# A conformer convolution whose last two channel tiles go partly to TensorE, with the layer norm's early work moved

## The chip, the core and the metric

The kernel runs on one core of a Trainium2 chip. The metric is the device time of one execution in microseconds (us). Before the change it is 2323.74 us, the median of three runs (2322.24 to 2327.69). TensorE (PE in the profile) multiplies matrices, VectorE (DVE), ScalarE (ACT) and GpSimd (POOL) work elementwise, and SyncE (SP) issues all the DMAs of this kernel from one queue.

## The reference

A trunk of two layers on 256 tokens of width 2048, float32. Layer 0 mixes tokens with a Conformer convolution module, layer 1 with stick-breaking attention; each is followed by a gated feed-forward network. Every sub-layer is normed, scaled and shifted by values made from the vector c. The change lies in layer 0's mixer:

```python
def ada_ln(c, w, b):
    mod = jax.nn.silu(c) @ w + b
    shift, scale, gate = jnp.split(mod, 3, axis=-1)
...
def conformer_conv_module(h, pw1_w, pw1_b, dw_w, dw_b, ln_g, ln_b, pw2_w, pw2_b):
    u = h @ pw1_w + pw1_b                        # 2048 -> 4096
    val, gt = jnp.split(u, 2, axis=-1)
    u = val * jax.nn.sigmoid(gt)
    u = causal_depthwise_conv(u, dw_w, dw_b)     # 31 taps per channel
    u = jax.nn.silu(layer_norm(u, ln_g, ln_b))   # over the 2048 channels
    return u @ pw2_w + pw2_b
```

## The kernel before

Activations lie transposed: 16 tiles (KD) of 128 channels x 256 tokens. The stretch in question runs from about 130 to 460 us of the profile and has four parts.

**The first product (pw1)** makes, for channel tile j, the value half and the gate half in one PSUM bank: 32 blocks of 128x128 weights per tile, 8 blocks to a "piece" of 0.5 MB. `gate_act(j)` (ACT, sigmoid) and `gate_mul(j)` (DVE) turn the bank into the tile `us[j]` (u).

**The convolution** has 31 taps. Tap 30 and the bias are one ACT instruction into PSUM (`conv_first`). The next 19 are DVE instructions that multiply and add onto it (`conv_tap`). The first 11 (`POOL_TAPS`) are products on ACT (`conv_prod`, into tiles named hl) that GpSimd adds into `ys[j]`. `conv_sum(j)` adds the two halves on DVE. A loop over c = 0..16 writes this out by hand, in steps s = 0..18: in round c stand the first half of tile c's taps, the second half of tile c-1's, `conv_sum(c-2)`, the pw1 pieces of later tiles and the sums below. Each engine executes its own instructions in the written order (`in_order`), so an instruction that waits holds up everything behind it on its engine.

**The layer norm over channels** needs sums over partitions, which TensorE makes by a product with ones (`y_sum`, `y_square_sum`). To avoid cancellation the tiles are first centred by an early mean m1 of the first M0 tiles: `gather("y0")` copies the partial sums to SBUF (ACT) and sums them (PE), `first_mean` makes m1 (ACT) and a correction dm (DVE), and `y_centre(j)` subtracts m1. After the last tile the exact mean and variance follow, then the normed tiles zh and zl (a float32 value split in two), the operands of the second product (pw2).

**Beside it** part of the scale, shift and gate values (`ada_ln`) is made on TensorE from rows of weights: a "row chunk" of 1 MB is loaded and used by four 128x32 matmuls (line 551, written to auxa), which the profile shows as 8 records. `mod_rows` is a generator; each `advance(fill, 1)` takes one chunk. `ROWS_AT` says at which (c, s) a chunk stands, `ROWS_TAIL` how many follow before pw2, and the rest is spread over the pieces of pw2 at the rate `RATES["pw2"]`. Chunk 16 ends the first group: its result is copied to SBUF by ACT ("rows", line 559). `ROWS` groups of columns of the feed-forward's shift are made from rows; the other column tiles (mt_ffn, 1 MB each) are made on DVE by one multiply-and-reduce each (`mod_reduce`, line 314), in the generator `mod_part`. Row chunks in pw2 and the mt tiles share three buffers, mraw.

In pw2 and after it a scheduler places the instructions. After pw2 the feed-forward's first product starts with 64 blocks (up00a), and the next (up00b) needs the normed tiles hh and hl that DVE, ACT and GpSimd make meanwhile.

The lines that the steps speak of (`y_sums` flushes the waiting tiles to TensorE):

```python
if c == M0 + 3:
    first_mean()
...
if s == 3 and c == M0 + 2:
    gather("y0")
...
if s == 10 and 1 < c < KD:
    y_sums(c - 2)
if s in (6, 10) and c > M0 + 2 and centred < JC:
    y_centre(centred)
```

Of the kernel before, what the change touches and what calls it, by code (L numbers as in the profile page):

```python
# [24 lines left out]
PRODUCTS = 16  # L25
# [4 lines left out]
M0 = 8  # L30
MORE_ROWS = 4
SPLIT_ROWS = 3
ROWS = 3

ROWS_AT = {**{c: (11,) for c in (2, 4, 6, 8, 10, 12)}, 13: (8, 13, 18), 14: (2, 6, 10, 14, 18), 15: (2, 6, 10, 14, 18), 16: (2, 4, 6, 7)}
ROWS_TAIL = 4

RATES = {"pw2": (0.65, 0.0), "up": (0.25, 0.25), "down": (0.4, 0.0), "qk": (0.3, 0.0), "v": (0.3, 0.0),
# [77 lines left out]
def hybrid_trunk(ctx: ExitStack, tc: tile.TileContext, cfg: Cfg, io: dict):  # L116
# [356 lines left out]
    with ExitStack() as cv:  # L473
# [119 lines left out]
        spare = [v[1] for v in htiles]  # L593
# [48 lines left out]
        conv_ps, conv_banks = {}, []  # L642

        def conv_first(j):
            if len(conv_banks) < 2:
# [3 lines left out]
                                 scale=tap(j, PADW))  # L649

# [13 lines left out]
        def conv_sum(j):  # L664
            nc.vector.tensor_tensor(ys[j], ys[j], conv_ps.pop(j), op=ALU.add)
# [12 lines left out]

        def gathered(ps):

            v = t256()
            nc.scalar.copy(v, ps[:, :T])
            return v
# [13 lines left out]
        def y_sums(j):  # L697

            waiting.append(j)
            if j in (3, 7, 11) or j >= KD - 3:  # L700
                while waiting:
                    y_sum(waiting.pop(0))

        def gather(name):

            v = gathered(st[name])
            nc.tensor.matmul(st[name][:, T:2 * T], ones_q, v, start=True, stop=name == "y0", skip_group_check=True)
# [6 lines left out]
        def y_centre(j):  # L714
            nc.vector.tensor_tensor(ys[j], ys[j], m1, op=ALU.subtract)
# [39 lines left out]
        for i in range(NH, KD):  # L755
            done = min(c for c in range(KD) if upto[c] + 2 >= (i - NH + 1) * per_pair)
            gates_at.setdefault(min(done + 2, i - 1), []).append(i)
# [7 lines left out]
        for c in range(KD + 1):  # L765
            late = gates_at.get(c, [])
            if c == M0 + 3:
                first_mean()
            squared, squares = [(j, y_square(j)) for j in squares], []
            if c < M0 + 4:  # L770
                load_rows()
            taps = [(c, s) for s in range(nd - nd // 2)] if c < KD else []
            if c > 0:
                old = [(c - 1, s) for s in range(nd - nd // 2, nd)]
                taps = [t for pair in zip(taps, old + [None]) for t in pair if t] if taps else old
            made = 0
            for s in range(nd):
                if s < len(taps):
                    j, k = taps[s]
                    conv_tap(j, POOL_TAPS + k)  # L780
                while c < KD and made < min(POOL_TAPS, (s + 1) * POOL_TAPS // (nd - 4) + 1):
# [16 lines left out]
                if s == 4:  # L798
# [3 lines left out]
                    if c == KD:  # L802
# [399 lines left out]
```

## Time and profile before

| | |
|---|---|
| runs | 2322.24, 2323.74, 2327.69 us |
| profiled execution | 2325.09 us, its span 2322.9 us |
| PE busy | 2277.3 us of the span |
| DVE, ACT, POOL busy | 1732.6, 1164.3, 263.2 us |
| moved by DMA | 603.55 MB, mean 260 GB/s |

The profiled execution is 2.2 us longer than its span, and 1.35 us above the median of the runs. Busy time of PE says little by itself, since matmuls overlap and the clock of PE changes; so the stretch is read by short windows, by the list of waits and by the timeline of each engine.

### The profile page before, as it was taken

Reading aid. Unit: us, or ns where it says so; the run is one execution under the profiler, and the core shown is the slowest. Engines: PE = TensorE matmul, PEld = TensorE weight load, DVE = VectorE, ACT = ScalarE, POOL = GpSimd, SP = SyncE. Lnnn points to the kernel's source line nnn. Section 1 sums busy time; section 2 is a strip of 40 time slices with the busy share of each in tenths; the row PEclk is TensorE's granted clock in tenths of the full one; section 3 lists DMA queues with packets and bytes.
Section 4 is the critical chain, followed back from the end, with each engine's and each line's share of the span. In section 5 each row is a group of like instructions: output and inputs, shape, how many; then the busy total and the mean of one; then the engine's idle time right before and its main releaser. Section 6 shows DMA issues by size and latency. Waiting matters only on the chain.

```text
span 2322.9 us, 44140 instructions
## 1 busy us (share of the span) xinstructions
PE 2277.3 (98%) x17850; PEld 2170.8 (93%) x17850; DVE 1732.6 (75%) x2389; ACT 1164.3 (50%) x1769; POOL 263.2 (11%) x339
## 2 busy tenths in 40 slices
PE   7999999999999999999999999999999999999997
PEld 5888578999999999999988999999999999999997
DVE  7688965988887788788876766888887545666554
ACT  2055565755543355554465555657555434555543
POOL 4057701200000000001111100111000000000010
PEclk9999899999999999999999999999999999999999
DMA  9988787587779877788866667775776555555553
GB/s 397 417 330 302 284 316 304 212 307 281 278 295 341 302 281 272 255 307 321 296 202 231 238 237 270 263 267 186 283 287 219 185 190 186 188 190 190 185 189 109
DMA packets 139166, 603.55 MB, mean 260 GB/s; under 512 B 15441, under 2 KB 15569, under 8 KB 115153
## 3 DMA queue, kind: packets, MB, share of 16 engines
q1 hardware_dynamic: 138962, 600.74, 71.3%
q8 instruction: 139, 2.28, 0.4%
q14 instruction: 65, 0.53, 0.1%
HBM read 598.58 MB, written 2.10 MB: 259 GB/s over the span
## 4 chain that ended last, share of the span: by engine, by line
PE 87%; DVE 7%; DMA 4%; ACT 1%; issue 1%; POOL 0%; SPq 0%; DVEq 0%; ACTq 0%; POOLq 0%
PE ps L286 25%; PE ps L287 25%; PE ps L288 25%; PE ps L629 4%; DMA mraw<-in_mt_mix 3%; DVE mraw L314 2%; PE auxa L551 2%; DVE wl L237 1%; PE ps L1034 1%; PE ps L1035 1%; PE ps L1036 1%; DVE auxb L652 1%; DMA mraw<-in_mt_ffn 1%; DVE hl L361 0%; DVE rstd L394 0%
## 5 line engine op out<-in xcount | busy, mean ns | idle before, releaser
L233 ACT CAST wh<-raw 128x1024 fp32r<-128x1024 f32 x688 | 720.8, 1048 | 799.8 <-PE ps L287 626.9
L237 DVE TENSOR_TENSOR wl<-raw,wh 128x1024 fp32r<-128x1024 f32 x688 | 840.6, 1226 | 362.0 <-ACT wh L233 355.0
L286 PE MATMUL ps<-hh,wh 128*128 128x256 f32 (+1 forms) x3328 | 935.4, 281 | 3.4 <-ACT hh L363 2.1
L287 PE MATMUL ps<-hl,wh 128*128 128x256 f32 (+1 forms) x3328 | 932.1, 280 | 0.0
L288 PE MATMUL ps<-hh,wl 128*128 128x256 f32 (+1 forms) x3328 | 927.6, 279 | 2.5 <-DVE wl L237 2.5
L287 PEld LDWEIGHTS ps<-hl,wh 128*128 128x128 f32 x3328 | 631.3, 190 | 0.3
L286 PEld LDWEIGHTS ps<-hh,wh 128*128 128x128 f32 x3328 | 626.0, 188 | 4.3 <-ACT hh L363 2.5
L288 PEld LDWEIGHTS ps<-hh,wl 128*128 128x128 f32 x3328 | 626.7, 188 | 2.8 <-DVE wl L237 2.7
L314 DVE CUSTOM_DVE_ANT_0 mraw<-mraw,csr 128x2048 f32<-128x2048 f32 x148 | 339.4, 2293 | 118.0 <-DMA mraw<-in_mt_mix 59.8
L287 PE MATMUL ps<-gl,wh 128*128 128x256 f32 x1408 | 395.6, 281 | 0.0
L286 PE MATMUL ps<-gh,wh 128*128 128x256 f32 x1408 | 394.4, 280 | 0.0
L288 PE MATMUL ps<-gh,wl 128*128 128x256 f32 x1408 | 393.1, 279 | 0.0
L287 PEld LDWEIGHTS ps<-gl,wh 128*128 128x128 f32 x1408 | 265.8, 189 | 0.0
L286 PEld LDWEIGHTS ps<-gh,wh 128*128 128x128 f32 x1408 | 265.0, 188 | 0.0
L288 PEld LDWEIGHTS ps<-gh,wl 128*128 128x128 f32 x1408 | 264.9, 188 | 0.0
L379 POOL TENSOR_TENSOR sumsq<-sumsq,t 128x256 f32<-128x256 f32 x56 | 58.4, 1044 | 1582.5 <-ACT t L375 1582.3
L629 PE MATMUL ps<-hh,raw 128*128 128x256 f32 x832 | 188.5, 382 | 0.0
L629 PEld LDWEIGHTS ps<-hh,raw 128*128 128x128 f32 x832 | 158.0, 191 | 27.8 <-issue 5.8
L899 DVE SCALAR_TENSOR_TENSOR t<-ps,par,t 128x254 f32<-128x254 f32 x336 | 160.5, 478 | 4.1
L652 DVE SCALAR_TENSOR_TENSOR auxb<-u,cpar,auxb 128x256 f32<-128x256 f32 x304 | 125.2, 482 | 11.2 <-ACT auxb L648 10.4
L786 POOL TENSOR_TENSOR y<-y,hl 128x256 f32<-128x256 f32 x144 | 106.8, 742 | 23.3 <-ACT hl L661 12.5
L896 ACT ACTIVATE t<-ps,par 128x256 f32<-128x256 f32 x168 | 93.9, 559 | 2.3 <-PE ps L288 2.3
(187 smaller groups left out, 2106.9 us busy)
## 6 DMA issues: line engine op xcount, KB each, us to landing
raw<-in_w_down SPq DMA_DIRECT2D x176, 512.0 KB, 4.0
mraw<-in_mt_mix SPq DMA_DIRECT2D x80, 1024.0 KB, 7.7
mraw<-in_mt_ffn SPq DMA_DIRECT2D x68, 1024.0 KB, 6.4
raw<-in_w_pw SPq DMA_DIRECT2D x96, 512.0 KB, 7.6
raw<-in_w_up01b SPq DMA_DIRECT2D x84, 512.0 KB, 5.0
raw<-in_w_up11b SPq DMA_DIRECT2D x84, 512.0 KB, 3.4
raw<-in_w_up00b SPq DMA_DIRECT2D x80, 512.0 KB, 4.8
raw<-in_w_up10b SPq DMA_DIRECT2D x80, 512.0 KB, 4.4
```

What stands on the lines that cost most here:

```text
L233: nc.scalar.copy(wh[:, :n], v[:, :n])
L237: nc.vector.tensor_tensor(wl[:, :n], v[:, :n], wh[:, :n].bitcast(F32), op=ALU.subtract)
L286: nc.tensor.matmul(o, wh[:, c], xh[kt], start=first, stop=False, skip_group_check=halves > 0)
L287: nc.tensor.matmul(o, wh[:, c], xl[kt], start=False, stop=False, skip_group_check=halves > 0)
L288: nc.tensor.matmul(o, wl[:, c], xh[kt], start=False, stop=left[nb] == 0, skip_group_check=halves > 0)
L314: nc.vector.tensor_tensor_reduce(out=v, in0=v, in1=csr, scale=1.0, scalar=0.0, op0=ALU.mult, op1=ALU.add, accum_out=macc[:, nb:nb + 1])
L379: engine.tensor_tensor(self.sum, self.sum, sq, op=ALU.add)
L629: nc.tensor.matmul(banks[j][:, nb // KD * T:(nb // KD + 1) * T], w[:, b * P:(b + 1) * P], hf[kt], start=first, stop=left[j] == 0, skip_gro ...
L652: nc.vector.scalar_tensor_tensor(conv_ps[j], us[j % UBUFS][:, k:k + T], tap(j, k), conv_ps[j], op0=ALU.mult, op1=ALU.add)
L786: nc.gpsimd.tensor_tensor(ys[c], ys[c], pr, op=ALU.add)
L896: nc.scalar.activation(y, ps[:, :T], AF.Identity, bias=pc(f"fdb{i}", nb, 1), scale=w(FW - 1))
L899: nc.vector.scalar_tensor_tensor(y[:, s:], ps[:, :T - s], w(k), y[:, s:], op0=ALU.mult, op1=ALU.add)
```

## The change

1. The last two channel tiles (`LATE` = 2, tiles 14 and 15) have 7 taps on GpSimd instead of 11 and 12 on DVE instead of 19; 11 taps are matmuls with diagonal matrices (`conv_tensor`), which ACT makes from an identity (`tap_matrix`), and one more DVE addition brings them in.
2. The first mean is taken of 6 tiles instead of 8. Its steps move: the sums to s = 4, the copy to (c, s) = (8, 12), `first_mean` to (9, 8). Eight early tiles (before ten) are centred late, and this is done on GpSimd.
3. `ROWS` 3 -> 2: 40 row chunks instead of 44, and eight mt tiles instead of four in this part of the shift. 22 chunks stand before or at the start of pw2 instead of 27. In pw2 the rate is 0.8 instead of 0.65, and the mt tiles are taken between the chunks instead of after them.
4. Product tiles of the convolution are 10 instead of 16 (`PRODUCTS`), the other six hl tiles hold tap matrices. The last gate stands at (14, 3) and (14, 5).

```diff
-PRODUCTS = 16
+LATE = 2
+LATE_POOL, LATE_PE = 7, 11
+PRODUCTS = 10
-M0 = 8
+M0 = 6
-ROWS = 3
-ROWS_AT = {... 13: (8, 13, 18), 14: (2, 6, 10, 14, 18), 15: (2, 6, 10, 14, 18), 16: (2, 4, 6, 7)}
-ROWS_TAIL = 4
-RATES = {"pw2": (0.65, 0.0), ...
+ROWS = 2
+ROWS_AT = {... 13: (8, 16), 14: (8, 10, 12, 14), 15: (2, 6, 8, 11), 16: (2,)}
+ROWS_TAIL = 5
+RATES = {"pw2": (0.8, 0.0), ...
@@ mods0
-            yield from mod_rows()
+            for _ in mod_rows():
+                yield
+                if nrow["bias"]:
+                    nrow["steps"] = nrow.get("steps", 0) + 1
+                    if nrow["steps"] > 5 and nrow["steps"] % 3 == 0:
+                        next(part, None)
             yield from part
@@
+        def tap_matrix(j, i, home):
+            diag[j, i] = home
+            nc.scalar.activation(home, ident, AF.Copy, scale=tap(j, PADW - LATE_PE + i))
+
+        def conv_tensor(j):
+            tens_ps[j] = psum_acc()[:, :T]
+            for i in range(LATE_PE):
+                k = PADW - LATE_PE + i
+                nc.tensor.matmul(tens_ps[j], diag.pop((j, i)), us[j % UBUFS][:, k:k + T], start=i == 0,
+                                 stop=i == LATE_PE - 1)
@@ conv_sum
+            if late_tile(j):
+                nc.vector.tensor_tensor(ys[j], ys[j], tens_ps.pop(j), op=ALU.add)
             nc.vector.tensor_tensor(ys[j], ys[j], conv_ps.pop(j), op=ALU.add)
@@ the loop over c and s
-            if c == M0 + 3:
-                first_mean()
-                if s == 3 and c == M0 + 2:
+                if (c, s) == (M0 + 2, 12):
+                    gather_copy("y0")
                     gather("y0")
+                if (c, s) == (M0 + 3, 8):
+                    first_mean()
-                if s == 10 and 1 < c < KD:
+                if s == 4 and 1 < c < KD:
                     y_sums(c - 2)
-                if s in (6, 10) and c > M0 + 2 and centred < JC:
-                    y_centre(centred)
+                if s in (6, 10) and c > M0 + 3 and centred < JC:
+                    y_centre(centred, nc.gpsimd)
...
+                if c == KD - 2 and s == 0:
+                    conv_tensor(KD - 2)
+                if c == KD - 2 and s == 3:
+                    sg = gate_act(KD - 1)
+                if c == KD - 2 and s == 5:
+                    gate_mul(KD - 1, sg)
...
+                if c == KD - 2 and s == nd - 1:
+                    conv_tensor(KD - 1)
```

How the instructions stand. First ACT around the early mean, before (rounds 10 and 11): hl are the convolution's products, auxb is `conv_first`, L682 the copy of the sums, L710 the mean m1.

```order
L682 COPY t<-ps 128x256
L661 ACTIVATE hl_1653<-u_254,cpar 128x256
L661 ACTIVATE hl_1657<-u_254,cpar 128x256
L661 ACTIVATE hl_1661<-u_254,cpar 128x256
L661 ACTIVATE hl_1676<-u_254,cpar 128x256
L661 ACTIVATE hl_1680<-u_254,cpar 128x256
L661 ACTIVATE hl_1684<-u_254,cpar 128x256
L648 ACTIVATE auxb<-u_255,cpar 128x256
L661 ACTIVATE hl_1696<-u_254,cpar 128x256
L661 ACTIVATE hl_1700<-u_254,cpar 128x256
L710 ACTIVATE m_271<-ps 128x256
```

The copy stands in front of `conv_first`(11), the mean after it. The same engine after the change, round 9 (the copy, L730, stands in round 8):

```order
L689 ACTIVATE hl_1585<-u_254,cpar 128x256
L689 ACTIVATE hl_1589<-u_254,cpar 128x256
L689 ACTIVATE hl_1604<-u_254,cpar 128x256
L738 ACTIVATE m_272<-ps 128x256
L689 ACTIVATE hl_1611<-u_254,cpar 128x256
L689 ACTIVATE hl_1615<-u_254,cpar 128x256
L664 ACTIVATE auxb<-u_255,cpar 128x256
```

The copy has moved some 1.5 rounds ahead; now the mean stands in front of the next `conv_first`, that of tile 10. On PE the second sum of the early mean (L734, formerly L707) stands behind the row chunk of round 8:

```order
L553 MATMUL auxa<-mrow,hot 32x512 x4
L734 MATMUL ps<-t,ones_q 128x256
L640 MATMUL ps<-hh_220,raw 128x256
L640 MATMUL ps<-hh_222,raw 128x256
L640 MATMUL ps<-hh_224,raw 128x256
```

Before, it stood between the second and third piece of round 10. Third, PE from the last pw1 block to the middle of the tail, after the change (u_259 and u_260 are the tiles 14 and 15, L676 their tap matmuls, L706 the column sums; x4 of L553 is one chunk):

```order
L640 MATMUL ps<-hh_250,raw 128x256
L553 MATMUL auxa<-mrow,hot 32x512 x4
L553 MATMUL auxa<-wh,hot 32x512 x2
L553 MATMUL auxa<-wl,hot 32x512 x2
L676 MATMUL ps<-u_259,hl_241 128x256 x2
L676 MATMUL ps<-u_259,hl_243 128x256 x2
L676 MATMUL ps<-u_259,hl_245 128x256 x2
```

```order
L553 MATMUL auxa<-mraw,hot 32x512 x4
L706 MATMUL ps<-t,ones_d 32x256
L706 MATMUL ps<-y_198,ones_d 32x256
L706 MATMUL ps<-y_199,ones_d 32x256
L706 MATMUL ps<-y_200,ones_d 32x256
L706 MATMUL ps<-y_201,ones_d 32x256
L553 MATMUL auxa<-mrow,hot 32x512 x12
L734 MATMUL ps<-t,ones_q 128x256
L718 MATMUL ps<-y_202,ones_d 128x256
```

Between the two pieces stand three sums, four chunks and tile 15's 11 tap matmuls. The three chunks in the second piece end with chunk 16. Between the last pw1 block and the first pw2 matmul there are 14 chunks (before: 21); 20 then follow inside pw2 (before: 17), by the 480th of its 768 matmuls (before: by the 672nd). ACT at the same place:

```order
L689 ACTIVATE hl_2170<-u_260,cpar 128x256
L561 COPY rows<-auxa 128x512
L689 ACTIVATE hl_2182<-u_260,cpar 128x256
L747 ACTIVATE t<-y_201 128x256
L235 CAST wh<-raw 128x1024
L730 COPY t<-ps 128x256 x2
```

The copy of chunk 16's result now stands ahead of the last product of tile 15, of a weight cast and of the two copies that the final sums on PE use.

More of the change, by code (lines that the diff above doesn't have):

```diff
@@ L29 @@
 UBUFS = 9
-M0 = 8
+M0 = 6
 MORE_ROWS = 4
 SPLIT_ROWS = 3
-ROWS = 3
-ROWS_AT = {**{c: (11,) for c in (2, 4, 6, 8, 10, 12)}, 13: (8, 13, 18), 14: (2, 6, 10, 14, 18), 15: (2, 6, 10, 14, 18), 16: (2, 4, 6, 7)}
-ROWS_TAIL = 4
-RATES = {"pw2": (0.65, 0.0), "up": (0.25, 0.25), "down": (0.4, 0.0), "qk": (0.3, 0.0), "v": (0.3, 0.0),
+ROWS = 2
+ROWS_AT = {**{c: (11,) for c in (2, 4, 6, 8, 10, 12)}, 13: (8, 16), 14: (8, 10, 12, 14), 15: (2, 6, 8, 11), 16: (2,)}
+ROWS_TAIL = 5
+RATES = {"pw2": (0.8, 0.0), "up": (0.25, 0.25), "down": (0.4, 0.0), "qk": (0.3, 0.0), "v": (0.3, 0.0),
          "o": (0.4, 0.0), "up00a": (0.0, 0.0), "qk0a": (0.0, 0.0),
@@ L592, in hybrid_trunk @@
         hf = [v[0][:, :T].bitcast(F32) for v in htiles]
-        spare = [v[1] for v in htiles]
+        spare = [v[1] for v in htiles[:PRODUCTS]]
+        homes_of_taps = [v[1][:, i:i + P].bitcast(F32) for v in htiles[PRODUCTS:] for i in (0, P)]
+        ident = homes_of_taps.pop()
+        nc.gpsimd.affine_select(out=ident, in_=ones, pattern=[[1, P]], compare_op=ALU.is_equal, fill=0.0, base=0,
+                                channel_multiplier=-1)
         act_tables("sigmoid_and_others")
@@ L699, in y_sums, with gather_copy @@
             waiting.append(j)
-            if j in (3, 7, 11) or j >= KD - 3:
+            if j in (3, M0 - 1, M0 + 3) or j >= KD - 3:
                 while waiting:
                     y_sum(waiting.pop(0))
+        def gather_copy(name):
+            st["g" + name] = t256()
+            nc.scalar.copy(st["g" + name], st[name][:, :T])
         def gather(name):
-            v = gathered(st[name])
-            nc.tensor.matmul(st[name][:, T:2 * T], ones_q, v, start=True, stop=name == "y0", skip_group_check=True)
+            nc.tensor.matmul(st[name][:, T:2 * T], ones_q, st.pop("g" + name), start=True, stop=name == "y0",
+                             skip_group_check=True)
         def first_mean():
@@ L778, in hybrid_trunk @@
                 if s < len(taps):
-                    j, k = taps[s]
-                    conv_tap(j, POOL_TAPS + k)
-                while c < KD and made < min(POOL_TAPS, (s + 1) * POOL_TAPS // (nd - 4) + 1):
+                    conv_tap(*taps[s])
+                while c < KD and made < min(pool_taps(c), (s + 1) * pool_taps(c) // (nd - 4) + 1):
                     pr = conv_prod(c, made)
```

37 lines of the change are left out of this document (25 added, 12 removed).

## The prediction

> **What bounds the kernel now.** The page shows PE busy in nearly every slice, so I read windows of 5 us from 130 to 460 us (columns: window, length, then busy time and instructions of PE, PEld, DVE, ACT and POOL, the granted clock as a share, the DMA share, GB/s) first, then the waits and the timelines of the engines where a window shows a hole.
>
> ```profile
> 225.00:230.00 5.00, 5.00 (x29) 3.81 (x28) 1.01 (x3) 0.31 (x2) 0.00 (x0) 1.00 0.72 286
> 270.00:275.00 5.00, 0.62 (x4) 0.18 (x2) 4.76 (x13) 1.16 (x4) 4.05 (x6) 0.86 1.04 421
> 275.00:280.00 5.00, 4.31 (x22) 1.28 (x20) 4.97 (x12) 4.52 (x13) 3.45 (x5) 0.50 1.02 387
> 280.00:285.00 5.00, 5.00 (x26) 2.60 (x26) 4.96 (x14) 3.15 (x8) 4.25 (x6) 0.50 0.97 388
> 285.00:290.00 5.00, 5.00 (x33) 1.66 (x28) 4.72 (x11) 0.00 (x0) 0.00 (x0) 0.77 1.03 433
> 300.00:350.00 50.00, 49.97 (x381) 40.01 (x384) 35.20 (x65) 30.43 (x50) 0.00 (x0) 1.00 0.87 335
> 435.00:440.00 5.00, 2.67 (x22) 2.43 (x20) 5.00 (x8) 4.73 (x9) 3.57 (x4) 1.00 0.18 70
> 440.00:445.00 5.00, 4.86 (x28) 4.86 (x29) 5.00 (x11) 3.03 (x8) 1.59 (x2) 0.66 0.48 150
> ```
>
> Only places where PE isn't full, or not at full clock, can give time back. At 225 DVE and ACT stand nearly still while PE is full: a stall that PE does not feel. Between 270 and 290 it is DVE that is full while PE has a hole and then half a clock. From 300 on pw2 fills PE. At 437 and after there is a second hole, again with half a clock behind it. The waits (total us, count, longest) say who is waited for, 225 to 300 first (where the copy L682 holds up ACT, and with it conv_first of tile 11), then 296 to 520:
>
> ```profile
> ACT t L682 <- PE ps L676: 16.9, 3, 9.7
> DVE auxb L652 <- ACT auxb L648: 7.9, 5, 6.9
> PE ps L676 <- ACT t L719: 4.4, 1, 4.4
> ```
> ```profile
> PE ps L288 <- DVE wl L237: 2.5, 1, 2.5
> PE ps L286 <- ACT hh L363: 1.1, 1, 1.1
> ```
>
> And the timelines (start, length) of PE and DVE:
>
> ```profile
> 220.80 1.07 PE L551 MATMUL auxa<-mrow,hot 128*32 128x512 f32 x8
> 228.90 0.64 PE L676 MATMUL ps<-y,ones_d 128*32 128x256 f32 x8
> 257.98 3.72 PE L629 MATMUL ps<-hh,raw 128*128 128x256 f32 x16
> 261.63 1.06 PE L551 MATMUL auxa<-mrow,hot 128*32 128x512 f32 x8
> 291.69 1.92 PE L551 MATMUL auxa<-mrow,hot 128*32 128x512 f32 x16
> 300.03 0.71 PE L286 MATMUL ps<-zh,wh 128*128 128x256 f32 x4 [1.35 <-ACT zh L360]
> 303.02 1.07 PE L551 MATMUL auxa<-mraw,hot 128*32 128x512 f32 x8
> ```
> ```profile
> 213.76 3.62 DVE L652 SCALAR_TENSOR_TENSOR auxb<-u,cpar,auxb 128x256 f32<-128x256 f32 x9
> 232.95 2.45 DVE L652 SCALAR_TENSOR_TENSOR auxb<-u,cpar,auxb 128x256 f32<-128x256 f32 x6 [6.94 <-ACT auxb L648]
> 290.71 0.42 DVE L715 TENSOR_TENSOR y<-y,m 128x256 f32<-128x256 f32 x1
> 295.25 0.42 DVE L841 TENSOR_TENSOR t<-ps,t 128x256 f32<-128x256 f32 x1
> ```
>
> PE ends pw1 at 261.63 and starts pw2 at 300.03. In between DVE sets the pace until tile 15 is centred at 291.13; the variance follows at 295.25, pw2 4.78 us later. So the length from 261.6 to 300.0, the chunks inside pw2 and the hole at 437 are what the change can move.
>
> **The change, part by part.**
>
> *The early mean.* The stall of 6.94 us before 232.95 goes from its place, but I expect it one round and a half earlier. The second sum of the mean (L734) now stands behind the row chunk of round 8, which PE reached at 220.80 before; PE is at L734 at 222.3 or so. DVE would reach the correction dm at about 215.7, in the middle of the nine taps that start at 213.76, and wait until about 223.4, 7.7 us. It then starts tile 11 at about 234.5, against 232.95. Behind DVE's wait stand taps only, and PE is held up by none of them before 262: 0 on the path, at most the 1.5 us of lateness if DVE stayed the bound.
>
> *DVE and POOL in the tail.* Durations from the groups of 255 to 300 (DVE) and 130 to 300 (POOL):
>
> ```profile
> L652 DVE SCALAR_TENSOR_TENSOR auxb<-u,cpar,auxb 128x256 f32<-128x256 f32 x66 | 27.9, 479 | 0.8 <-ACT auxb L648 0.5
> L715 DVE TENSOR_TENSOR y<-y,m 128x256 f32<-128x256 f32 x11 | 6.3, 570 | 0.2
> L786 POOL TENSOR_TENSOR y<-y,hl 128x256 f32<-128x256 f32 x144 | 106.8, 742 | 23.3 <-ACT hl L661 12.5
> ```
>
> DVE loses 2 x 7 taps at 27.9/66 = 0.42 us (5.9) and eight centrings at 0.57 (4.6) and gains two additions (0.8): 9.7 less, 1.5 late, so tile 15 is summed at about 282 to 283 instead of 291. POOL gains eight centrings, for which I take 0.74 each: twelve operations in a round of tile 10 or later are 9 us, a round of DVE is 9 us too, so POOL runs level, and the late tiles give it back 2 x 4 additions. Nothing waits for it longer than before by this count.
>
> *PE from pw1 to pw2.* Piece prices: a chunk is half of the 1.92 us at 291.69 less 0.2 for the trailing end, 0.87; a 128x256 product in float32 is 3.72 less 0.2 for eight, 0.44, which I take for a tap product, as its shape is the same. One group of sums more stands ahead of the last piece (the group at 228.90, 0.6 to 1.0): 262.6. Two chunks: 264.3. Eleven taps of tile 14: 269.1. Sums and four chunks: 273.1. Eleven taps of tile 15: 277.9, if ACT has its tap matrices ready. Those are 22 small ACT copies without a row; between the per-piece price of the tiny casts and of the copy below they cost 0.10 to 0.37, 2 to 8 us against 2 x 4 products saved at 0.41 (3.3); I take 0.25 (the size lies between), which has them done at 272.6, just in time, and the bad end makes PE 2 us later. Then a chunk, five sums and three chunks: 282.1. Here PE waits, because the ACT copy that feeds L734 now stands behind the result of chunk 16:
>
> ```profile
> 405.52 1.12 ACT L437 CAST hh<-v_ffn 128x2 fp32r<-128x2 f32 x11
> 278.23 0.58 ACT L559 COPY rows<-auxa 128x512 f32<-128x512 f32 x1 [0.48 <-PE auxa L551]
> 254.08 4.09 ACT L661 ACTIVATE hl<-u,cpar 128x256 f32<-128x256 f32 x10
> 281.72 0.42 ACT L719 ACTIVATE t<-y 128x256 f32<-128x256 f32 x1 [0.29 <-DVE y L715]
> 282.04 1.03 ACT L233 CAST wh<-raw 128x1024 fp32r<-128x1024 f32 x1
> 229.69 0.37 ACT L682 COPY t<-ps 128x256 f32<-128x256 f32 x1 [9.70 <-PE ps L676]
> 286.95 0.84 PE L707 MATMUL ps<-t,ones_q 128*128 128x256 f32 x2
> ```
>
> Copy of the rows, last product, square, cast, copy: 0.58 + 0.41 + 0.42 + 1.03 + 0.37 = 2.8, so L734 starts at 285.0, PE idle for 2.9. Then L734 (0.84) and, as before from the centring of tile 15 to the variance, 295.25 - 291.13 = 4.1: variance at 289.9, pw2 at 294.8. That is **-5.2**, at full clock.
>
> *The clock.* The hole of 4.38 us before left the clock at 0.86, 0.50, 0.50 and 0.77 in four windows, 1.37 x 5 = 6.9 us of a full clock. At 437 a shorter hole (2.47) gave 0.66 in one window, 1.7 us. The new gap of 2.9 lies nearer the shorter one, but sparse column sums follow it: bounds 0 and 5, taken **+2.5**.
> [...]
>
> *Chunks inside pw2.* 20 instead of 17, at 1.07 to 1.1 (303.02): **+3.3**. That is the only lasting cost of moving seven chunks behind the norm, as four of them are gone altogether.
>
> *Transfers in pw2.* PE's chunks in 300 to 350, the chunk loads in 255 to 430 (transfers, size, median us from issue to landing), and SP's waits there:
>
> ```profile
> L551 PE MATMUL auxa<-mraw,hot 128*32 128x512 f32 x61 | 11.2, 605 | 0.0
> mraw<-in_mr_ffn SPq DMA_DIRECT2D x20, 1024.0 KB, 7.5
> SPq L215 <- PE auxa L551: 79.8, 20, 9.4
> ```
>
> The fastest rows above (270, 285) moved 421 and 433 GB/s. Before, pw2 ran at 335 (row 300) and PE never waited for a load. A product costs 0.13 us: the 381 records of row 300 are 61 of 7.6 chunks, 8 small ones and 312 products, and 49.97 - 7.6 x 1.07 - 1 = 40.8. After the change, from the third chunk of pw2 to the 480th product stand loads of 16 chunks (1.05 MB), 5 mt tiles and 15 weight pieces (0.52 MB), 29.9 MB or 71 us at 420 GB/s, against 480 x 0.13 + 17 x 1.07 = 80 us of PE. But ten chunks stand between the 300th and the 480th product, 180 x 0.13 + 10.7 = 34 us of PE, and with three mt tiles and eight pieces they load 17.8 MB, 42 us, through three mraw buffers of which an mt tile holds one until DVE has reduced it. If nothing were loaded ahead, 8 us would be missing there and some 4 more from buffers that come free late: bounds 0 and 12. The load share of 0.87 at row 300 leaves little reserve, but the queue can load ahead up to its buffers: I take **+4**, a third of the way.
>
> *The hole at 437.* It comes from the mt reductions late in pw2, which hold up DVE ahead of the reciprocal of the next norm:
>
> ```profile
> 413.23 2.28 DVE L314 CUSTOM_DVE_ANT_0 mraw<-mraw,csr 128x2048 f32<-128x2048 f32 x1
> 422.97 0.47 ACT L392 ACTIVATE t<-auxb,eps_r 128x256 f32<-128x256 f32 x1 [1.99 <-PE auxb L384]
> 427.08 1.74 DVE L394 RECIPROCAL rstd<-t 128x256 f32<-128x256 f32 x1
> ```
>
> The root is ready at 423.4, the reciprocal starts 3.6 us later. After the change chunks and mt tiles are through at the 480th product of 768, some 37 us before pw2 ends, so the reciprocal starts at once: the 2.47 and the 1.7 of half clock go, **-4.1**. The 1.1 behind it waits for ACT and I leave it; with it the bound is -5.2, and 0 if DVE is late for another reason.
>
> The sum: -5.2 + 2.5 + 3.3 + 4 - 4.1 = **+0.5**. The profiled execution (2325.09 us, 2.2 outside its span) is 1.35 above the median, so 2325.6 there and **2324.2** on the scale of the median.
>
> **The rivals.**
>
> *Loads keep up and the gap is harmless* (faster). [...] -5.2 + 0 to 1 + 3.3 + 0 to 1 - 4.1 = -6 to -4.9, about 2318, down to 2316.6 with the 1.11 too. Against it: 0.87 of the engines' time is used already at a lower rate of chunks.
>
> *pw2 is bound by its loads* (slower). Place: the last ten chunks before the 480th product. Price: 9 to 12 instead of 4, so +5.5 to +8.5, and where the half clock returns during the waits 2 more: about 2331. It decides once fewer than about 8 us of work are loaded ahead when chunk 30 is due. For it: 42 us of transfers against 34 of PE. Against it: the reserve before.
>
> [...]
>
> *The stall isn't removed at all* is part of the forecast, since PE doesn't feel it either way.
>
> **How the numbers follow.** About 0.2% (4.6 us) is what a measurement of this kernel can tell from no change. Forecast 0.36, full clock gate 0.07: both within; loads keep up 0.31, faster; loads bind 0.26, slower. The likeliest alone runs from 2320 to 2328. The range for eight in ten takes most of both rivals, leaving out the far tail of each: 2315.5 to 2333.
>
> **What would show it.** Right: pw2's first product near 295 to 297; a stall of DVE of 6 to 8 us near 216 to 223, on the second use of m1; a PE gap of 2 to 4 us near 283 behind the copy of the rows; no wait for wl at the end of up00a; 20 chunks by the 480th product with single PE waits for mraw or raw that sum to about 4. Wrong: pw2 as late as 300 (tap matrices or u of tile 15 late, or a half clock through the whole tail); PE waits for loads of over 8, or none; the hole at 437 still there; POOL's centrings so slow that sums wait for them.

## The result and the profile after

The changed kernel takes 2346.82 us (median of 4 runs, 2344.18 to 2351.08) against 2324.58 beside it: a ratio of 1.0088, 95% interval 1.0074 to 1.0102. It is slower by 20.5 us by the ratio and 22.2 by the medians, where 2324.2 was forecast with a range up to 2333.0. The profiled execution took 2344.18 us, its span 2342.1, 19.2 more than before.

Windows of after, with the columns of the prediction (window, length, then busy time of PE, PEld, DVE, ACT and POOL, the granted clock, the DMA share, GB/s):

```profile
285.00:290.00 5.00, 3.66 (x22) 1.94 (x22) 1.27 (x3) 1.25 (x4) 0.24 (x1) 1.00 1.01 428
295.00:300.00 5.00, 2.83 (x22) 0.93 (x14) 4.44 (x7) 2.52 (x5) 0.00 (x0) 0.87 0.73 252
340.00:380.00 40.00, 32.27 (x245) 23.86 (x243) 20.63 (x31) 17.25 (x33) 8.98 (x8) 1.00 0.76 287
380.00:420.00 40.00, 34.74 (x217) 27.99 (x218) 21.07 (x28) 15.23 (x27) 2.50 (x3) 0.74 1.00 403
420.00:440.00 20.00, 20.00 (x173) 20.00 (x173) 18.81 (x31) 12.73 (x27) 5.08 (x4) 1.00 0.54 185
```

The same stretch of before, in one row:

```profile
340.00:420.00 80.00, 80.00 (x648) 68.35 (x648) 51.03 (x78) 47.80 (x87) 13.44 (x14) 1.00 0.80 308
```

Before, PE had neither a hole nor a slow clock between 340 and 420. After, it stands idle for 7.7 + 5.3 = 13.0 us there, and the clock is down to 0.74 in the second half; by windows of 5 us (0.56, 0.50, 0.91, 0.77, 0.50 and 0.71 from 380 to 410, each times PE's busy time) that is, by estimate, some 8.5 us of a full clock. From 340 to 380 the DMA engines are not full either (0.76), from 380 to 420 they are (1.00). So nearly the whole loss lies in the second half of pw2. PE's timeline of after tells who is waited for (a choice of rows, with the longest waits; in square brackets the idle time and who ended it):

```profile
285.94 0.70 PE L734 MATMUL ps<-t,ones_q 128*128 128x256 f32 x2 [2.64 <-ACT t L730]
297.69 0.71 PE L288 MATMUL ps<-zh,wh 128*128 128x256 f32 x4 [2.17 <-ACT zh L362]
378.19 1.07 PE L553 MATMUL auxa<-mraw,hot 128*32 128x512 f32 x8 [2.36 <-DMA mraw<-in_mr_ffn]
380.70 1.94 PE L553 MATMUL auxa<-mraw,hot 128*32 128x512 f32 x8 [1.44 <-DMA mraw<-in_mr_ffn]
397.77 1.94 PE L553 MATMUL auxa<-mraw,hot 128*32 128x512 f32 x8 [2.59 <-DMA mraw<-in_mr_ffn]
464.70 0.36 PE L288 MATMUL ps<-hh,wh 128*128 128x256 f32 x1 [1.69 <-DVE bcol L465]
475.84 0.62 PE L288 MATMUL ps<-hh,wh 128*128 128x256 f32 x3 [0.98 <-ACT hh L365]
```

The first two are the holes ahead of pw2. The next three are row chunks that had not landed, 6.4 of the 13.0 us. The rest of the 13.0 are ten waits of 0.2 to 1.3 us: 3.5 us for weights (wh, which ACT rounds from raw, and wl, which DVE makes behind it) and 2.9 for ACT, which empties the accumulators of finished tiles and copies a result of chunks. The weights' loads came late too: ACT waited for them twice for 5 us. And the load queue itself stood still, for 9 us between two chunk loads. ACT's timeline, the queue's, and the queue's waits in 300 to 400 (total, count, longest):

```profile
381.94 1.04 ACT L235 CAST wh<-raw 128x1024 fp32r<-128x1024 f32 x1 [5.08 <-DMA raw<-in_w_pw]
387.72 1.05 ACT L235 CAST wh<-raw 128x1024 fp32r<-128x1024 f32 x1 [4.74 <-DMA raw<-in_w_pw]
```
```profile
356.94 8.97 SPq L217 DMA_DIRECT2D mraw<-in_mr_ffn  x2
```
```profile
SPq L217 <- PE auxa L553: 61.3, 17, 5.6
SPq L217 <- DVE macc L316: 15.2, 4, 8.2
```

The first of these rows for before, in the same stretch (the second has no counterpart there):

```profile
SPq L215 <- PE auxa L551: 53.6, 12, 9.4
```

SP issued all loads in one order. Loads of chunks waited until PE had used the chunk before the last (L553, 61.3 us), loads of an mt tile or of the chunk behind it until DVE had reduced an mt tile (L316, 15.2 us), and the weights written behind them waited too: none were issued from 352.5 to 376.3. The 9 us at 356.94 are such a wait for DVE (8.2). DVE reached the reduction at 363.27 only, since in its order it first waited for the scale (2.95 us, until 358.68) and then had the tiles to do that the scale releases. The DMA engines were at 0.19 from 360 to 365, and full again from 375 to 380:

```profile
375.00:380.00 5.00, 1.89 (x16) 0.16 (x8) 3.35 (x4) 1.31 (x3) 0.72 (x1) 1.00 0.99 386
```

Three places show where the 19.2 us were lost. The first product of pw2 starts 2.3 us earlier than before (297.69 against 300.03), its last ends 22.5 us later (438.76 against 416.30), and the 300th product behind pw2 starts 19.8 us later (478.46 against 458.67). So pw2 took 24.8 us longer, 2.7 were gained behind it, and no more was lost after that.

### The profile page after: what moved, and what is told of

The parts are those of the page before. It is cut to its first block, busy times and chain, and to the rows that moved or that the text cites. A ratio compares the mean times of both kernels' runs of the same rounds, so it can differ in the third digit from the quotient of the medians.

```text
span 2342.1 us, 44146 instructions
## 1 busy us (share of the span) xinstructions
PE 2284.2 (98%) x17862; PEld 2177.2 (93%) x17862; DVE 1732.5 (74%) x2377; ACT 1166.9 (50%) x1783; POOL 264.3 (11%) x340
## 4 chain that ended last, share of the span: by engine, by line
PE 85%; DVE 6%; DMA 6%; issue 2%; ACT 1%; SPq 0%; POOL 0%; DVEq 0%; ACTq 0%; POOLq 0%
PE ps L288 25%; PE ps L289 25%; PE ps L290 24%; PE ps L640 5%; DMA mraw<-in_mt_mix 3%; DVE mraw L316 2%; DVE wl L239 2%; PE auxa L553 1%; DMA mraw<-in_mt_ffn 1%; PE ps L1084 1%; PE ps L1085 1%; PE ps L1086 1%; DMA mraw<-in_mr_ffn 1%; DVE hl L363 0%; DMA raw<-in_w_pw 0%
## 5 line engine op out<-in xcount | busy, mean ns | idle before, releaser
L235 ACT CAST wh<-raw 128x1024 fp32r<-128x1024 f32 x688 | 720.5, 1048 | 792.3 <-PE ps L289 618.1
L316 DVE CUSTOM_DVE_ANT_0 mraw<-mraw,csr 128x2048 f32<-128x2048 f32 x152 | 348.4, 2292 | 128.9 <-DMA mraw<-in_mt_ffn 66.3
L288 PEld LDWEIGHTS ps<-gh,wh 128*128 128x128 f32 x1408 | 264.9, 188 | 0.0
L680 DVE SCALAR_TENSOR_TENSOR auxb<-u,cpar,auxb 128x256 f32<-128x256 f32 x290 | 118.8, 483 | 4.9 <-ACT auxb L664 4.1
L815 POOL TENSOR_TENSOR y<-y,hl 128x256 f32<-128x256 f32 x136 | 99.3, 730 | 28.1 <-ACT hl L689 15.6
```

The costliest lines, as they stand in the source:

```text
L235: nc.scalar.copy(wh[:, :n], v[:, :n])
L288: nc.tensor.matmul(o, wh[:, c], xh[kt], start=first, stop=False, skip_group_check=halves > 0)
L316: nc.vector.tensor_tensor_reduce(out=v, in0=v, in1=csr, scale=1.0, scalar=0.0, op0=ALU.mult, op1=ALU.add, accum_out=macc[:, nb:nb + 1])
L680: nc.vector.scalar_tensor_tensor(conv_ps[j], us[j % UBUFS][:, k:k + T], tap(j, k), conv_ps[j], op0=ALU.mult, op1=ALU.add)
L815: nc.gpsimd.tensor_tensor(ys[c], ys[c], pr, op=ALU.add)
```

## The experiments

Each was timed beside the kernel before; the ratio to it is given with its interval. The edits are shown shortened, `...` marking what is left out. Line numbers shift by a few between the kernels: L286 to L292 are the products, L551 to L555 the chunks, L233 or L235 ACT's rounding of weights. "Planner" is the scheduler's order on PE, "program" the order in which the program is written. "Product" counts the 768 products of pw2, in the order in which PE's trace has them: the first tile of pw2 is finished at the 300th, and the code asks there for the feed-forward's whole scale, whose last row chunk is the 32nd, with two steps (two more chunks) behind it. The 32nd stands at the 192nd product before, at the 344th after.

| run | chunks before pw2, rate, PE's order in pw2 | 32nd chunk | ratio (95%) |
|---|---|---|---|
| after | 22, 0.8, planner | 344 | 1.0088 (1.0074 to 1.0102) |
| mt_after | 22, 0.8, planner, mt tiles last | 334 | 1.0062 (1.0046 to 1.0079) |
| reduce_next | 22, 0.8, planner | 344 | 1.0086 (1.0071 to 1.0101) |
| rate65 | 22, 0.65, planner | 383 | 1.0053 (1.0035 to 1.0071) |
| near25 | 25, 0.8, planner | 269 | 1.0067 (1.0051 to 1.0084) |
| near27 | 27, 0.8, planner | 193 | 1.0056 (1.0044 to 1.0068) |
| near27_65 | 27, 0.65, planner | 207 | 1.0017 (1.0008 to 1.0025) |
| near28t | 28, 0.8, planner | 167 | 1.0038 (1.0026 to 1.0049) |
| cap3 | 22, 0.8, planner, 3 buffers | 322 | 1.0105 (1.0091 to 1.0119) |
| pe_order | 22, 0.8, program | 300 | 1.0044 (1.0029 to 1.0059) |
| pe_order25_65 | 25, 0.65, program | 264 | 1.0018 (1.0008 to 1.0027) |
| pe_order_near25 | 25, 0.8, program | 216 | 0.9996 (0.9987 to 1.0006) |
| after_27 | 27, 0.65, program | 192 | 0.9999 (0.9990 to 1.0008) |
| pe28t | 28, 0.8, program | 120 | 0.9997 (0.9987 to 1.0007) |
| pe28t_65 | 28, 0.65, program | 168 | 0.9982 (0.9974 to 0.9991) |
| tail_only | as before | as before | 1.0026 (1.0015 to 1.0037) |
| before_mods | before with the rows' part | 334 | 1.0105 (1.0084 to 1.0126) |
| before_22 | before with 22 chunks | 353 | 1.0063 (1.0046 to 1.0080) |
| rows2_27 | before, two groups, program | 192 | 1.0016 (1.0003 to 1.0028) |

**Which half of the change.** Two runs split it.

```diff
 # tail_only: after, with the row chunks of before
-ROWS = 2
+ROWS = 3
-ROWS_AT, ROWS_TAIL, RATES["pw2"] and mods0 of after
+those of before
```

> The first part of the change alone: taps on TensorE, six-tile mean, centring on GpSimd, with the row chunks as before (44 chunks, 27 before pw2, rate 0.65, four mt tiles after the chunks). All theories that put the loss into pw2's loads: pw2 runs as before, without PE waits. PE then has 21 chunks and 22 tap products after the last pw1 block, seven chunks at 0.87 more than after, of which some fill the gap of 2.6: pw2 starts at 300 to 303 instead of 297.7, so the time is that of before or up to 3 us more, 2323 to 2328. A theory by which the taps or the centring cost the 20 us would have 2340 or more.

Ratio 1.0026, and no loss in the loads: the window from 340 to 420 is full, at a clock of 1.00.

```profile
340.00:420.00 80.00, 80.00 (x647) 67.48 (x647) 47.34 (x71) 45.43 (x85) 14.09 (x14) 1.00 0.80 301
```
```profile
300.60 1.20 PE L288 MATMUL ps<-zh,wh 128*128 128x256 f32 x4 [3.08 <-ACT zh L362]
438.13 0.58 PE L288 MATMUL ps<-hh,wh 128*128 128x258 f32 x1 [3.39 <-ACT wh L235]
```

pw2 starts at 300.60 against 300.03: with the same chunks, the relief of DVE buys nothing, because the 22 tap products (2 x 5.0 us) fill what PE had idle (4.38 us ahead of 274.80) and at half clock (0.50 from 275 to 285) before. The hole at the end of up00a is a little longer (3.39 against 2.47). The 6 us are more than expected. Most of them are there by the 300th product behind pw2, which starts 5.2 us later than before (463.92 against 458.67): 0.6 ahead of pw2, 2.6 inside it (about 1.7 of this is clock, at 0.91 from 300 to 320) and 2.1 behind it.

```diff
 # before_mods: before, with the rows' part of the change
-ROWS = 3
+ROWS = 2
+ROWS_AT, ROWS_TAIL, RATES["pw2"] and mods0 of after
```

> The second part of the change alone, on the kernel before: two row groups instead of three, 22 row chunks before pw2 instead of 27, rate 0.8, mt tiles between the chunks; the convolution and the centring as before. If the loss lies in pw2's loads: pw2 starts near 300 as before (DVE sets the tail) and loses the same 20 us and more, 2342 to 2350. If the loss came from the tail's changes: near 2325.

Ratio 1.0105: the rows' part alone has the whole loss (the intervals of the two overlap). Its trace has 12.0 us of idle PE between 340 and 420, against 13.0 in after and none before. So the loss comes with the rows' part and lies in pw2.

**Do the mt tiles hold the buffers?**

```diff
 # mt_after: after, in mods0
-            for _ in mod_rows(): yield; ... next(part, None)
+            yield from mod_rows()
             yield from part
```

> The kernel after, with one thing undone: the eight mt tiles of the feed-forward's shift are again taken after the row chunks and not between them; everything else (taps on TensorE, two row groups, rate 0.8) stays. Theory H (held buffers): an mt tile sits in one of the three mraw buffers until DVE reduces it one mt step later (10.7 to 18.8 us in the trace after), the load queue stops behind it, and weights and chunks come late. Then the PE waits of 350 to 400 us (12.8 us, and about 10 us of half clock behind them) go, and the hole at the end of up00a (about 4 us) may return: 2324 to 2330. Theory R (row chunks alone are too many too soon: 20 by the 480th product through two buffers, three of them in a row): the waits for chunks stay, 2338 to 2345.

```diff
 # reduce_next: after, mod_part reduces one step after its load
-                    if nrow["steps"] > 5 and nrow["steps"] % 3 == 0:
+                    if nrow["steps"] > 5 and nrow["steps"] % 3 in (0, 1):
```

> The kernel after, with the same loads in the same order, but each mt tile is reduced on DVE one chunk step after its load instead of three. Theory H (buffers held by unreduced mt tiles stop the load queue): a tile is held some 8 us less, most of the waits in 350 to 400 go, 2328 to 2336. Theory R (row chunks alone are too many too soon): no change within 3 us, 2344 to 2350. A third possibility, that DVE itself is held up by a reduction whose tile has not landed, would make it slower than after.

mt_after: 1.0062. PE's idle time in 340 to 420 falls from 13.0 to 5.8 and the clock there rises to 0.96, but the mt tiles now end at 442, and PE waits for the shift:

```profile
445.94 0.80 PE L288 MATMUL ps<-hh,wh 128*128 128x258 f32 x2 [7.67 <-ACT hh L439]
```

So the mt tiles between the chunks are part of the loss, and moving them back loses most of it again. reduce_next: 1.0086, no change; its trace says why it tells nothing. DVE's reductions stand at 339.85, 364.82 and 379.08, as in after (338.25, 363.27, 377.53): each is 1.5 us later, as is the start of pw2 (299.31 against 297.69, 1.6 later). The experiment did not change what it meant to change.

**Is it the rate, the lateness of the scale, or the planner's order?** Four runs, of which each takes away one cause, and the last all three:

```diff
 # rate65: after
-RATES = {"pw2": (0.8, 0.0), ...
+RATES = {"pw2": (0.65, 0.0), ...
 # near25: after
-15: (2, 6, 8, 11), 16: (2,)}
+15: (2, 6, 8, 11, 12, 13, 14), 16: (2,)}
 # pe_order: after
+        here = len(nc.cur_bb.bb.instructions)
         gemm("pw2", ..., pw2_done, halves=8)
+        in_order(here, (nc.tensor.engine,))
 # pe_order25_65: the three together
```

> The kernel after with 25 row chunks before pw2 instead of 22: three more stand behind chunk 16, in the 2.6 us in which PE waits for ACT, and 18 are left for pw2; mt tiles between the chunks, rate 0.8. Theory B (burst): the first finished tile of pw2 (about the 300th product) needs the whole scale, that is 32 chunks; with 22 before pw2 they are not there yet, so the missing ones are loaded one behind the other through two buffers and the weights behind them in the queue come late. With 25 nothing is missing at that point: most of the 12.8 us of PE waits and 10 us of half clock go, 2325 to 2330. Theory Q (the rate of 0.8 with mt tiles between asks for more than the queue can move): waits stay, 2338 to 2345. Theory P (the planner puts chunks on PE ahead of where their loads stand in the queue): waits partly stay, since three chunks still stand together near the 450th product, 2333 to 2342.

> The kernel after with one number undone: the rate of row chunks in pw2 is 0.65 again instead of 0.8; two row groups, 22 chunks before pw2, mt tiles between the chunks. Theory Q (the rate asks too much of the queue): 2326 to 2334. Theory B (burst of chunks that the first finished tile needs): the burst is one chunk longer, the waits stay or grow, 2343 to 2352. Theory P (planner's order on PE against the order of the loads): four chunks stand together on PE instead of three, 2343 to 2352 too.

> The kernel after, with PE's instructions inside pw2 kept in the order in which the program writes them (the loads already are), so no chunk stands on PE ahead of the place that its load has in the queue; the three chunks that the first finished tile asks for stand together at the 300th product. Theory P: the waits for chunks go, 2326 to 2334. Theory B: the burst and the queue's order are the same, the waits only move ahead to the 300th product, 2340 to 2350. Theory Q: the same waits, 2340 to 2350.

> Three things together: PE in the program's order inside pw2, 25 chunks before pw2, rate 0.65. By each of the theories B, P and Q its own cause is gone, so all expect no PE wait of weight in pw2: the start of pw2 as after or 1 us later, 18 chunks, the hole at the end of up00a gone or shorter if the mt tiles end early enough: 2318 to 2327. If waits of 5 us and more remain, the cause is a fourth one (the mt tiles' hold on the buffers).

Each alone gives back a part, 5 us (near25, at the edge of what the two intervals can tell), 8 (rate65) and 10 (pe_order), and none the whole; the three together 16. So B (the burst), Q (the rate) and P (the planner's order) all failed as single causes. What they left over is instructive. With 25 chunks DVE still stood for 7.3 us in front of the addition that finishes the scale, with everything behind it in its order:

```profile
346.89 0.19 DVE L574 TENSOR_TENSOR v_ffn<-ps,par 128x16 f32<-128x16 f32 x1 [7.26 <-PE ps L568]
```

With PE in the program's order one wait for a chunk of 5.5 us is left, at the 300th product, where the missing chunks (32nd to 34th) are fetched together, beside three short waits for ACT (2.9 in all):

```profile
354.65 1.93 PE L555 MATMUL auxa<-mraw,hot 128*32 128x512 f32 x8 [5.52 <-DMA mraw<-in_mr_ffn]
```

**Does fetching them together cost by itself?**

```diff
 # before_22: before, ROWS = 3, rate 0.65, mt tiles last
-ROWS_AT = {... 13: (8, 13, 18), 14: (2, 6, 10, 14, 18), 15: (2, 6, 10, 14, 18), 16: (2, 4, 6, 7)}
-ROWS_TAIL = 4
+ROWS_AT = {... 13: (8, 16), 14: (8, 10, 12, 14), 15: (2, 6, 8, 11), 16: (2,)}
+ROWS_TAIL = 5
```

> The kernel before with one thing changed: 22 row chunks before pw2 instead of 27 (the places of the change), all else as before: three row groups, rate 0.65, mt tiles after the chunks, the old convolution. DVE sets the tail, so pw2 starts near 300 as before, and five more chunks in pw2 cost 5 us. Theory B (burst): the first finished tile of pw2 asks for the whole scale, six chunk loads stand one behind the other in the queue (none so in the kernel before), through two buffers; PE waits there for 5 to 10 us and half a clock follows: 2338 to 2348. If a burst does no harm: 2330 to 2334.

Ratio 1.0063: five chunks fewer ahead of pw2 cost the old kernel 15 us. The queue's timeline and PE's waits (300 to 480):

```profile
342.68 22.58 SPq L215 DMA_DIRECT2D mraw<-in_mr_ffn  x6
```
```profile
PE ps L286 <- ACT wh L233: 6.7, 2, 4.7
PE ps L288 <- DVE wl L237: 0.8, 1, 0.8
```

Six chunk loads stand one behind the other for 22.6 us, and no weights pass meanwhile; in the kernel before, no two chunk loads follow each other between 327 and 384. PE then waits for weights, not for chunks. But only 3.0 us of these waits lie in pw2, fewer than the 5 to 10 expected; the longest, 4.7, is the hole at the end of up00a (at 449), which was 2.5 before. Of the 14.9 us that are lost by the 300th product behind pw2, 1.5 lie ahead of pw2, 11.6 in it and 1.8 behind it. The 11.6 are 5.3 for the five chunks' own time, 3.0 of waits and some 3.3 of clock (0.95 from 340 to 380, 0.92 from 380 to 400). So the loads that stand together cost the old kernel about 6 us.

```diff
 # pe_order_near25: near25 and pe_order together, rate 0.8
 # after_27: program order, rate 0.65
+15: (2, 6, 8, 11, 12, 13, 14, 15, 16), 16: (2,)}
 # rows2_27: before, program order, mt tile at every second step
-ROWS = 3
+ROWS = 2
```

> PE in the program's order inside pw2, 25 chunks before pw2, rate 0.8, mt tiles between the chunks: no two chunk loads stand together in the queue. Beside the earlier run at 0.65, which had two loads together at the 300th product and still waited 4.9 us there. Theory B (the burst is what costs): 2323 to 2329, no single wait for a chunk over 2 us. Theory Q (rate of 0.8 with mt tiles between asks too much): 2332 to 2338.

> The kernel after with 27 chunks before pw2, rate 0.65, PE in the program's order inside pw2: the new convolution with no burst of loads. pw2 starts later than after by the five chunks less the gaps that they fill, near 300.5 as in the run of the first part alone; 16 chunks in pw2 and no waits of weight. Theory B: 2321 to 2327. If the mt tiles between chunks hold the queue: 2328 to 2334.

> The kernel before, its convolution untouched, with the part of the change that saves work and without the part that delays chunks: two row groups instead of three (13 chunks in pw2 instead of 17), 27 chunks before pw2 as before, rate 0.65, PE in the program's order inside pw2, an mt tile at every second chunk from the fourth on, so that no chunks stand together in the queue and all are through by the 480th product. Theory B: no waits in pw2, 4 chunks less (-4), hole at the end of up00a gone (-4): 2318 to 2322. If an mt tile between chunks costs waits by itself: 2325 to 2332.

With no loads standing together at the 300th product and PE in the program's order, the loss can no longer be measured: 0.9996 and 0.9999 (in their traces the 300th product behind pw2 is 1.7 and 2.4 us later than before). Against pe_order25_65 (1.0018), which is slower at the lower rate because two loads meet at the 300th product again, this speaks for the meeting and against the rate. rows2_27 missed: 1.0016, where a gain of 4 to 8 was expected. At the 300th product behind pw2 its trace is only 0.7 us ahead of before (457.99 against 458.67), since PE stood idle for 5.6 us in pw2, in four waits for ACT to empty accumulators, and the clock fell to 0.96 from 340 to 380. Its span is still 9.7 us longer; 8.5 us of that come in layer 1, around its attention, between 1321 and 1600 us of before. The same stretch is up to 3.9 us longer than before in the traces of the other runs, though no edit touches it, so a single trace does not tell how much of this is the edit's.

**Is the number of chunks enough, without PE in order?**

```diff
 # near27: after
+15: (2, 6, 8, 11, 12, 13, 14, 15, 16), 16: (2,)}
 # near27_65: the same, rate 0.65
 # near28t: near25, and
-ROWS_TAIL = 5
+ROWS_TAIL = 8
```

> The kernel after with one thing undone, the number of row chunks before pw2: 27 instead of 22 (five more behind chunk 16). Rate 0.8, mt tiles between the chunks, the planner's order on PE and the new convolution stay. The last chunk of the scale (the 32nd) then stands at about the 193rd product of pw2 instead of the 344th, with its two later steps by the 269th; the first finished tile needs the scale at the 300th. Theory D (deadline: what costs is that the scale is not ready when the first tile of pw2 is finished, so that ACT and DVE wait in order and hold up the weights, and the missing chunks are fetched together): most of the loss goes, 2325 to 2331, no single wait of DVE for the scale. Theory P (planner's order on PE, with mt tiles between): as with 25 chunks, 2337 to 2343.

> As the run with 27 chunks before pw2, and the rate 0.65 instead of 0.8. Theory D: the scale's last chunk stands at the 207th product, its later steps by the 283rd, just in time; within 3 us of the run at 0.8. Theory Q (the rate with mt tiles between asks too much): faster than at 0.8 by 5 us or more.

> The kernel after with 28 chunks before pw2: three behind chunk 16, in PE's wait for ACT, and three more at the end, in PE's wait of 3 us for the first normed tile. Theory D: the scale's last chunk at the 167th product, no waits for it; the six chunks fill two gaps, so pw2 starts at 299 to 300 with 15 chunks inside: 2321 to 2328, the likeliest of these to be faster than the kernel before (up to 3 us).

No: 1.0056 with 27, so theory D (the lateness of the scale) fails as the only cause. With the rate of 0.65 as well it is 1.0017. At 0.8 PE waits for weights, though behind 310 us no two chunk loads stand together:

```profile
357.14 0.39 PE L288 MATMUL ps<-zh,wh 128*128 128x256 f32 x1 [1.90 <-ACT wh L235]
380.91 0.39 PE L288 MATMUL ps<-zh,wh 128*128 128x256 f32 x1 [1.83 <-ACT wh L235]
```

In the planner's order of near27 the chunks that the program writes at the 216th, 240th and 336th product stand on PE at the 269th, 312th and 402nd; in the kernel before, up to the 480th product, none stands behind its place in the program. The queue issues nothing for 6.3, 5.7 and 6.6 us ahead of the chunk loads at 361.97, 368.47 and 375.84, each with weights behind it. That chunks used later free their buffers later and so make the weights late, and that a higher rate leaves less room for this, fits the waits and the two ratios, but was not shown. near28t, with the scale earlier still, is between (1.0038); its twelve times fall into two groups of six, 2328.7 to 2333.7 and 2337.0 to 2340.3, and its trace is of the first. Three pairs of runs differ in PE's order alone: near25 and pe_order_near25 (1.0067 and 0.9996), near27_65 and after_27 (1.0017 and 0.9999), and near28t with pe28t of the next step (1.0038 and 0.9997). In each the program's order is the faster (the intervals of the second pair just touch).

**More buffers, and the conditions together.**

```diff
 # cap3: after
-                cap = {"m": 3 if near else 2, ...
+                cap = {"m": 3 if near else 3, ...
 # pe28t: near28t and pe_order;  pe28t_65: the same, rate 0.65
```

> The kernel after with one number changed: row chunks in pw2 may hold all three mraw buffers instead of two, so each chunk is loaded one chunk earlier. All else, 22 chunks, rate 0.8, mt tiles between, the planner's order, stays. Theory S (the load queue stands still behind a chunk whose buffer PE has not freed, and the weights behind it come late): a chunk load waits for a use that lies one chunk further back, so about half of the loss goes, 2332 to 2340. If the mt tiles need the third buffer, the queue stops at them instead: 2343 to 2350.

> 28 row chunks before pw2 (three in PE's wait for ACT, three in its wait for the first normed tile) and PE in the program's order inside pw2, rate 0.8, mt tiles between, the new convolution. Theory S: chunks stand on PE in the order and at the places of their loads, the scale is ready in time, no waits for loads; pw2 starts at 298.5 with 15 chunks instead of 17, no hole at the end of up00a, but single waits of PE for ACT at the first finished tiles (about 4 us together, as in the runs with PE in order): 2320 to 2327.

> As the run before it with rate 0.65. Theory S: the same within 3 us, 2320 to 2328; slower only if the mt tiles then end so late that the hole at the end of up00a returns.

cap3 is not faster than after, 1.0105 (the intervals overlap). Its queue stands in front of the same pair of loads (363.61, 8.50 us), waiting for DVE's reductions (12.4 us in 300 to 400, the longest 7.8): the chunks have taken the buffer that the mt tiles need. pe28t is as fast as before, and pe28t_65 is the one version whose interval lies below 1: 2324.29 against 2328.06, 0.9982 (0.9974 to 0.9991), a gain of 0.2% that is the best of 19 versions. Its PE, before pw2 and in 340 to 420:

```profile
298.57 0.35 PE L290 MATMUL ps<-zh,wh 128*128 128x256 f32 x1 [0.66 <-ACT zh L364]
```
```profile
340.00:420.00 80.00, 75.24 (x606) 67.68 (x606) 62.31 (x89) 46.33 (x91) 17.49 (x14) 0.98 0.81 314
```

The wait for zh has fallen from 2.17 to 0.66, since three chunks stand in it, and the 4.8 us of idle time left in pw2 are four waits for ACT to empty the accumulators of finished tiles.

## Why the prediction was wrong

*The term that failed* is the transfers in pw2: +4, with bounds of 0 and 12. In its place the trace has 13.0 us of idle PE and about 8.5 of clock, 21.5 together. The working compared megabytes with PE's time, found 42 us of loads against 34 of PE at the end, and added some 4 us for buffers that come free late: 12 at worst, and no clock. The trace shows another way for the loss to arise. From 340 to 380, where the first 7.7 us of idle time lie, the DMA engines were busy for 0.76, which is the mean of a stretch without work and a full one: 0.19 from 360 to 365 (PE idle for 2.4 us), while the one queue stood behind a load without a buffer, and 0.99 from 375 to 380 (PE idle for 3.1), when the loads held back came together. That the one brought the other is read off the trace; no run isolates it. The prediction had rows of the queue's waits (79.8 us of SP waiting for PE's chunks) and took them for a reserve. Their sum does not tell a reserve from a loss: from 300 to 400 it is 53.6 us before and 61.3 after, but from 330 to 385 it is 43.8 before, 34.1 after and 28.9 in pe_order_near25, which lost nothing, with 12.4 (after) and 12.5 (pe_order_near25) of waits for DVE's reductions. What differs is which loads stand behind the wait, and when PE needs them. The prediction's clock term covers the gap before pw2 alone, while the waits for loads inside pw2 were followed by a slower clock too: 0.56 and 0.50 (380 to 390) behind those at 378 and 381, 0.50 (400 to 405) behind the one at 398.

*A dependence was missed.* Moving chunks behind the norm was priced as chunk time. The prediction does not say that the first finished tile asks for the whole scale, and so for the 32nd chunk by the 300th product. before_22 shows the price of that in the old kernel: about 6 us in pw2 on top of the 5 for the chunks.

*The rival that came nearest* is "pw2 is bound by its loads" (0.26). It had the place right, as the three waits for chunks stand among the last ten before the 480th product, but gave 2331 for a time that is 2346.8, and its 2 us of half clock were 8.5. In the rival on the other side, in which the loads keep up, the sum of -6 to -4.9 comes out as -6 to -4.0; nothing else rests on it. No run shows the source of its 0 to 1 for the clock: in after the clock was full behind the gap of 2.64 us, as the chance of 0.07 had it, but cost about 1.5 us behind the gap in front of pw2 (295 to 310), and in cap3 it fell behind the first one too (0.68 and 0.50).

*The other steps.* DVE's stall on the early mean: forecast 7.7 us to 223.4, on DVE's timeline of after

```profile
223.96 0.42 DVE L739 SCALAR_TENSOR_TENSOR dm<-m,ps 128x256 f32<-128x256 f32 x1 [7.86 <-ACT m L738]
285.28 0.42 DVE L694 TENSOR_TENSOR y<-y,ps 128x256 f32<-128x256 f32 x1 [1.15 <-POOL y L815]
292.92 0.42 DVE L891 TENSOR_TENSOR t<-ps,t 128x256 f32<-128x256 f32 x1 [0.73 <-PE ps L758]
```

it is 7.86, and PE did not feel it. The taps of tile 14 began at 264.9 (264.3) and those of tile 15 at 273.9 (273.1), in time with their tap matrices; PE's gap before L734 was 2.64 (2.9). Tile 15 was summed at 286.2 instead of 282 to 283, 1.15 of that for POOL, which was not hidden. The variance came at 292.9 instead of 289.9: a chunk and the turn of chunk 16's result stand on PE between the last sums (287.0 to 289.0), and only the bare chain of before was counted. So pw2 began at 297.69, 2.3 earlier instead of 5.2. The clock's term of +2.5 was about 1.5 (0.87 in the 5 us from 295, 0.89 in the 10 us from 300, each times PE's busy time), 1.1 of it behind that start, so the two together gave -1.2 instead of -2.7. The chunks inside pw2 were 20, as counted (+3). The hole at 437 went as forecast (-4.1), but up00b has a new wait of 1.69 for DVE, and gained 2.6.

Summed up: -1.2 + 3 + 13.0 + 8.5 - 2.6 = 20.7 against 19.8 measured at the 300th product behind pw2. The 0.9 too many may be clock time in which PE would have waited for loads anyway; that was not shown.

*What is settled and what is not.* Shown: the loss is in the rows' part (before_mods, tail_only), it is in the waits between 340 and 420 and the clock behind them, fewer chunks ahead make a loss by themselves (before_22), and it goes when the chunks are early and PE uses them at the places where their loads stand in the queue (pe_order_near25, after_27, pe28t). At the rate of 0.8 both are needed: 1.0088 with neither, 1.0067 with 25 chunks, 1.0044 with the program's order, 0.9996 with both. Argued and not shown: that the way from these two to PE's waits leads through the queue standing at a load without a buffer. The traces fit it, and so does mt_after, where the mt tiles leave the buffers to the chunks and PE's idle time in 340 to 420 falls from 13.0 to 5.8 us; but reduce_next and cap3, which aimed at the buffers too, did not free them. Open: how much of the loss of rows2_27 behind pw2 is due to its edit.

## What to carry to other kernels

In this kernel one queue issued the loads for several pools of buffers, and while a load waited for its buffer (8.2 us for DVE at 356.94 in after) the loads behind it were held up: price the move of a load by what stands behind it in the queue and by when its buffer comes free, not by bytes against bandwidth. Before work is moved later, look up who asks for its result first, and count the loads that stand together at that point. Compare two traces at the same product, not at the same kind of wait, which can move to another place in the order. An undo that gives back only a part is no proof against a cause; with three conditions it took pairs to see it.

## What the runs showed of the hardware

The same gap did not always cost the same clock. Up to the start of pw2, after and cap3 have the same instructions on PE and the same idle time of 2.64 us before L734, and yet the clock behind it was 1.00 in after (the window of 285 above), but in cap3 it fell:

```profile
285.00:290.00 5.00, 4.16 (x18) 2.11 (x18) 1.27 (x3) 0.78 (x2) 0.14 (x1) 0.68 1.01 426
290.00:295.00 5.00, 4.54 (x13) 3.11 (x13) 0.69 (x2) 2.65 (x5) 0.00 (x0) 0.50 1.02 431
```

and pw2 began at 300.76 instead of 297.69. Of six profiled kernels with this same lead-in three began near 297.6 (after, rate65, pe_order) and three between 299.3 and 300.8 (reduce_next, mt_after, cap3). So with the same gap of 2.64 us ahead, pw2 began early or 1.7 to 3.2 us later, though nothing ahead of it differs in the order on PE: from 285 to 290 the clock was 1.00 in the three early ones and 0.66 to 0.71 in the three late ones. A single profile does not tell which is usual. The second gap, the one in front of pw2 (1.6 to 2.2 us in the six), was followed by a slower clock in all but cap3 (1.00 from 300 to 340): 0.79 from 300 to 305 in after, and 0.91 to 0.97 from 300 to 320 in the other four.
